# A hybrid decoder trunk: the sampled rows' mixers at the end of the mixing stage, the gating's gate half ahead of its other half

## The chip, the cores and the metric

One Trainium2 chip; the kernel runs on one of its cores. The metric is the device time of one execution in microseconds (us), the median of three runs. One launch computes two layers for 512 prompt rows and for 32 sampled rows (8 sequences of 4 tokens with 2048 cached positions each).

## The reference

Each layer normalises x, projects it from 1024 to 2048 columns, hands these to four mixers of width 256, joins their outputs in one projection of 1024 to 1024, and adds the normalised result to x. A SwiGLU network of inner width 2816 follows.

```python
def hybrid_layer(x, pos, conv_prev, pool_prev, attend, lam_init, p):
    h = rms_norm(x, p['g_mix_pre'])
    z = h @ p['w_in']
    a, ga, u, vb, q, k, v, xd = jnp.split(z, IN_SPLITS, axis=-1)
    ya, conv_new = conformer_conv(a, ga, conv_prev, p['conv_w'], p['conv_b'], p['conv_ln_g'], p['conv_ln_b'])
    yb, v_rows = chunk_sgu(jax.nn.gelu(u, approximate=False), jax.nn.gelu(vb, approximate=False),
                           p['sgu_w'], p['sgu_b'], p['sgu_ln_g'], p['sgu_ln_b'])
    o = attend(q, k, v, lam)
    yc = (rms_norm(o, p['attn_sub_g'], LN_EPS) * (1.0 - lam_init)).reshape(B_, T, D_C)
    yd, pool_new = pool_mix(xd, pool_prev, pos, p['pool_w'], p['pool_scale'])
    mix = jnp.concatenate([ya, yb, yc, yd], axis=-1) @ p['w_out']
    x = x + rms_norm(mix, p['g_mix_post'])
    gate, up = jnp.split(rms_norm(x, p['g_ffn_pre']) @ p['w_gu'], 2, axis=-1)
    x = x + rms_norm((jax.nn.silu(gate) * up) @ p['w_down'], p['g_ffn_post'])
```

`conformer_conv` is a causal depthwise convolution of 31 taps over `a * sigmoid(ga)`, a LayerNorm and a swish; `chunk_sgu` multiplies u by a 128x128 lower-triangular mixing of the LayerNormed v, plus a bias; `attend` is differential attention, for the sampled rows over their paged cache; `pool_mix` takes means over 2, 4, 8 and 16 positions. The sampled rows continue from `state_conv` (30 rows) and `state_pool` (15 rows) of each sequence.

## The kernel before, in words

Everything is float32, and each product of two float32 matrices is three matmuls of rounded parts (`whi`/`wlo` for weights, `xhi`/`xlo` or `y` for activations; L194 on ScalarE casts the high part of a 128x1024 piece, L197 takes the low part on VectorE, some on GpSimd). Program order per engine is fixed beforehand by a scheduler that lists the generated instructions by their data and by a priority; `urgent` flows get a higher one.

A layer has two stages.

**Mixing** (`mixing`): the input projection runs as 16 units of 24 matmuls, in blocks of 256 columns in the order of the list `order` (conv's two halves, k, q, v of attention, the pooling's 1792, the gating's u at 512 and v at 768). Prompt columns are 256 wide per half, and each second half carries the 32 sampled rows too (288 wide), evicted into `zs`. While blocks come in, the mixers run as generator flows that `advance` steps: `conv` (60 tap steps, L427, on VectorE, then transposes L450, LayerNorm, L458, L460 to L462), `attention`, `gating` (weights `wn` transposed by L578 and masked into `wt`, bias by `wt,sgr`; Gelu L593 and L594 over both halves; v transposed by L600 and LayerNormed into `vn` by L602; product `wt,vn`; L612 and L615 finish it) and `pooling`. The hi/lo halves of the results, `ya`, `yb`, `yc`, `yd`, are made by L351 and L352. PSUM is split among the tags `ps` (3 banks), `acc` (2), `s` (2) and `oT` (1); `gating`'s products use `acc`.

**Feed-forward** (`prompt` as main flow, `sample` in the background): `project_last` multiplies by w_out in eight turns of 24 matmuls 128x512, (token tile, half) in the order of `W_OUT_TURNS`, the 128-row pieces of the 1024 in the order of `W_OUT_ORDER`. The matmuls of the first turns stand in program order among the last steps of the mixing stage, as their `y` and weights come. Each turn ends in a copy L1285, a square L1289 and, on GpSimd, a product with the gain L1290; after the second half of a tile `finish` makes its norm (L1300, the root by L177 and L178, L1308, the square L1313, L1315) and turns it feature-major (L239, L241, L242), from which w_gu and w_down are computed. When all four tiles are turned, `share["turned"]` is set.

`sample` first steps `sample_conv`, `sample_gate` and `sample_pool` in a pool of their own, `smx`. `sample_conv` builds the 34 rows of each sequence in `scx` and adds 31 taps for two channel halves on VectorE: two steps L883 and 60 steps L886 of 128x32 per layer, and then a LayerNorm (L892 to L902). With `turned`, `sample_attention` opens its own pool, loads its tables (`sc`, `se`, `gsub`), spreads the queries (`rep`, `qs` by 32 copies L958), computes the new keys' scores, and then goes through the pages: gathers `kr` (L1000) and `vr` (L1030) by indirect DMA from GpSimd's queue, transposes `kt` (L1003) on VectorE, products `sx<-kt,qs` on TensorE. `sample_ffn` follows.

The lines that the steps below touch, word for word:

```python
W_OUT_ORDER = (6, 7, 0, 1, 2, 3, 4, 5)
            for f in (2, 0):
                S.activation(uv[:, f:f + 2], uv[:, f:f + 2], AF.Gelu)
            S.activation(zs[:, 4:8, :], zs[:, 4:8, :], AF.Gelu)
                V.scalar_tensor_tensor(a[:, c], ext[:, c, :, t:t + 4], pf[:, 8 + 2 * t + c:9 + 2 * t + c], a[:, c],
                                       op0=ALU.mult, op1=ALU.add)
```

## Time and profile before

| | us |
|---|---|
| median of three runs | 1465.84 (1464.1 to 1468.32) |
| the profiled execution, its own time | 1470.1 |
| its span | 1468.2 |
| TensorE busy | 1393.0 (95%) |
| VectorE busy | 816.3 (56%) |
| ScalarE busy | 490.4 (33%) |
| GpSimd busy | 253.9 (17%) |

All rows below are from this one execution; their times count from the start of its span. A busy TensorE is not one at its peak, as the ends of its matmuls are modelled. The granted clock (PEclk) is a share of full speed, in which one level is 2.4 GHz and the other 1.2 GHz.

### The profile page before, as it was taken

The page shows a single profiled execution, that of the slowest core. Times are in us where ns is not written, and L with a number is a line of the kernel's source. Part 1 is how long each engine was busy: PE and PEld are TensorE (multiplying, and loading weights), DVE is VectorE, ACT ScalarE, POOL GpSimd, SP SyncE. Part 2 cuts the span into 40 slices and gives each one's busy share as a digit, 9 for nine tenths or more (in the row PEclk, how much of TensorE's full clock was granted, in tenths as well). Part 3 has the DMA queues.
Part 4 walks back from the last instruction along what each step waited for, and adds up shares of the span by engine and source line. Part 5 has one row for each costly group of instructions (what it writes and reads, how often), then busy time and mean ns, then how long its engine had stood idle before and what let it go on. Part 6 is the DMA issues. An engine that isn't in the chain of part 4 may idle for free.

```text
span 1468.2 us, 22964 instructions
## 1 busy us (share of the span) xinstructions
PE 1393.0 (95%) x9274; PEld 1085.7 (74%) x9274; DVE 816.3 (56%) x1624; ACT 490.4 (33%) x972; POOL 253.9 (17%) x271
## 2 busy tenths in 40 slices
PE   6999798989999999999989997989899999999997
PEld 6988677856676777777779886787566677777775
DVE  4997577866424323433669856867564333333344
ACT  4345444322224221222333464433222332222231
POOL 1000245443300000000210004434342000000003
PEclk9999998999999999999999999999999999999999
DMA  6220336786859731323432213378767596213132
GB/s 206 93 87 30 131 117 213 257 299 230 286 177 292 238 137 58 104 69 128 152 115 73 73 53 109 128 244 299 274 235 266 182 299 210 100 58 115 58 133 90
DMA packets 155204, 235.60 MB, mean 160 GB/s; under 512 B 8880, under 2 KB 116410, under 8 KB 155098
## 3 DMA queue, kind: packets, MB, share of 16 engines
q1 hardware_dynamic: 136522, 166.76, 34.8%
q0 software_dynamic: 18432, 67.12, 12.8%
q8 instruction: 73, 1.20, 0.3%
q14 instruction: 33, 0.27, 0.1%
q10 hardware_dynamic: 144, 0.26, 0.0%
HBM read 222.07 MB, written 12.04 MB: 159 GB/s over the span
## 4 chain that ended last, share of the span: by engine, by line
PE 73%; DVE 8%; issue 7%; DMA 6%; POOL 3%; ACT 2%; another core or an unknown queue 0%; SPq 0%; POOLq 0%; DVEq 0%; ACTq 0%
PE acc L128 57%; PE sx L128 8%; DMA kr<-in_cache_k_dram,ik 4%; PE ps L128 2%; PE s L128 2%; DVE sca L886 2%; POOL vr L1030 1%; DVE wlo L197 1%; PE oT L128 1%; POOL kr L1000 1%; DVE m L1315 1%; ACT whi L194 1%; POOL rsw L178 1%; DMA rws<-in_w_gu_dram 1%; PE ps L518 1%
## 5 line engine op out<-in xcount | busy, mean ns | idle before, releaser
L128 PE MATMUL acc<-xhi,whi 128*128 128x512 f32 (+2 forms) x1152 | 409.5, 357 | 3.7 <-issue 1.7
L128 PE MATMUL acc<-xlo,whi 128*128 128x512 f32 (+2 forms) x1152 | 406.7, 353 | 4.2 <-DVE xlo L242 3.2
L128 PE MATMUL acc<-xhi,wlo 128*128 128x512 f32 (+2 forms) x1152 | 407.1, 354 | 0.4 <-issue 0.2
L197 DVE TENSOR_TENSOR wlo<-raw,whi 128x1024 fp32r<-128x1024 f32 x172 | 216.6, 1265 | 198.8 <-ACT whi L194 193.0
L194 ACT CAST whi<-raw 128x1024 fp32r<-128x1024 f32 x178 | 184.3, 1048 | 362.9 <-PE acc L128 320.8
L128 PEld LDWEIGHTS acc<-xhi,whi 128*128 128x128 f32 x1152 | 219.7, 191 | 47.5 <-issue 14.2
L128 PEld LDWEIGHTS acc<-xlo,whi 128*128 128x128 f32 x1152 | 219.9, 191 | 35.8 <-issue 5.7
L128 PEld LDWEIGHTS acc<-xhi,wlo 128*128 128x128 f32 x1152 | 219.6, 191 | 34.6 <-issue 7.9
L128 PE MATMUL acc<-whi,h 128*128 128x512 f32 x704 | 224.7, 396 | 0.6 <-issue 0.6
L128 PEld LDWEIGHTS acc<-whi,h 128*128 128x128 f32 x704 | 131.3, 188 | 44.5 <-issue 11.2
L128 PE MATMUL acc<-wlo,h 128*128 128x512 f32 x352 | 138.4, 395 | 0.0
L1290 POOL TENSOR_TENSOR m<-m,g_g_ffn_post 128x512 f32<-128x512 f32 x14 | 20.2, 1449 | 511.2 <-ACT junk L1289 511.2
L1003 DVE STREAM_TRANSPOSE kt<-kr 128x1024 f32<-128x1024 f32 x64 | 78.3, 1234 | 47.4 <-DMA kr<-in_cache_k_dram,ik 26.9
L1000 POOL DMA_INDIRECT kr<-in_cache_k_dram,ik x64 | 70.3, 1099 | 109.8 <-DVE kt L1003 85.3
L427 DVE SCALAR_TENSOR_TENSOR cacc<-hext,pf,cacc 128x512 f32<-128x512 f32 x120 | 86.9, 745 | 0.8
L128 PEld LDWEIGHTS acc<-wlo,h 128*128 128x128 f32 x352 | 66.1, 188 | 18.0 <-issue 4.6
L1030 POOL DMA_INDIRECT vr<-in_cache_v_dram,iv x64 | 60.5, 945 | 84.7 <-PE sx L128 67.0
L1359 DVE SCALAR_TENSOR_TENSOR th<-th,acc 128x512 f32<-128x512 f32 (+1 forms) x46 | 29.6, 644 | 78.9 <-PE acc L128 78.9
L178 POOL TENSOR_TENSOR rsw<-rsw,mhalf 128x1 f32<-128x1 f32 (+2 forms) x62 | 38.5, 628 | 172.0 <-DVE rsw L177 169.1
L128 PE MATMUL sx<-kt,qs 128*32 128x128 f32 x1024 | 49.3, 278 | 9.3 <-issue 8.6
L554 POOL TENSOR_TENSOR rse<-e,mhalf 128x8 f32<-128x8 f32 x4 | 7.5, 1879 | 257.4 <-DVE e L552 257.4
L1361 ACT CAST h<-th 128x512 fp32r<-128x512 f32 (+1 forms) x48 | 27.9, 582 | 66.5 <-DVE th L1359 58.9
(422 smaller groups left out, 1835.9 us busy)
## 6 DMA issues: line engine op xcount, KB each, us to landing
...
```

The lines of the kernel that those rows point to most:

```text
L128: T.matmul(out, lhsT, rhs, start=start, stop=stop)
L178: G.tensor_tensor(y, v, mhalf[:P, :n], op=ALU.pow)
L194: S.copy(hi, src)
L197: eng.tensor_tensor(lo, src, hi.bitcast(F32), op=ALU.subtract)
L427: V.scalar_tensor_tensor(a, hext[c][:, t:t + SEQ], pf[:, 8 + 2 * t + c:9 + 2 * t + c], a, op0=ALU.mult, op1=ALU.add)
L886: V.scalar_tensor_tensor(a[:, c], ext[:, c, :, t:t + 4], pf[:, 8 + 2 * t + c:9 + 2 * t + c], a[:, c], op0=ALU.mult, op1=ALU.add)
L1000: G.indirect_dma_start(out=kr, out_offset=None, in_=ck, in_offset=bass.IndirectOffsetOnAxis(ap=ik[:, s, bg:bg + 1], axis=0))
L1003: V.transpose(kt, kr)
L1030: G.indirect_dma_start(out=v.rearrange("p t e -> p (t e)"), out_offset=None, in_=cv, in_offset=bass.IndirectOffsetOnAxis(ap=iv[:, s, a:a + ...
L1290: (V if (t, half) == (3, 1) else G).tensor_tensor(m[t][:, hs], m[t][:, hs], gain[:, hs], op=ALU.mult)
L1359: V.scalar_tensor_tensor(th[:, :n], th[:, :n], 0.5, ou[:, :n], op0=ALU.mult, op1=ALU.mult)
L1361: S.copy(hh, th[:, :n])
```

## The change

It has four parts.

1. The gating's v half (block 768) is projected ahead of the pooling's 1792, and u (512) last. `gating` starts after v: Gelu of v alone, LayerNorm, product; then it waits for "u", takes u's Gelu, and finishes. Its weights `wn` are loaded into the tile of the norm, "xn", whose other user `vn` comes later. The conv's flow becomes urgent for its tail.
2. `sample_conv`, `sample_gate` and `sample_pool` run at the end of `mixing`, in tiles that attention no longer needs (its `q` and `k` tiles and the ring "p"). Their six loads per layer go out from GpSimd's queue in place of SyncE's. The 62 steps by taps become four products 128x496 (windows by taps), four reductions over the taps, and two additions of the bias.
3. A new pool `sqa` holds what the sampled attention needs before the pages: `sample_queries` makes `rep`, the new keys' scores and `onew` before "turned"; `sample_attention` keeps the `qs` copies and the pages.
4. `W_OUT_ORDER` starts with attention's pieces (4, 5) and has the gating's (2, 3) last.

```diff
-W_OUT_ORDER = (6, 7, 0, 1, 2, 3, 4, 5)
+W_OUT_ORDER = (4, 5, 0, 1, 6, 7, 2, 3)
...
+            (768, [(6, ev_copy(uv[:, 2], 6)), (7, ev_copy(uv[:, 3], 7))]),
             (1792, [(14, ev_copy(dext[0], 14, 1.0, 15)), (15, ev_copy(dext[1], 15, 1.0, 15))]),
             (512, [(4, ev_copy(uv[:, 0], 4)), (5, ev_copy(uv[:, 1], 5))]),
-            (768, [(6, ev_copy(uv[:, 2], 6)), (7, ev_copy(uv[:, 3], 7))]),
...
+            urgent.append(flow["conv"])
+            yield
             o = ps()
...
-            wn = mp.tile([128, 4, 128], F32, tag="t512", bufs=3, name="wn")
+            wn = mp.tile([128, 4, 256], F32, tag="xn", bufs=1, name="wn")[:, :, :128]
...
-            for f in (2, 0):
-                S.activation(uv[:, f:f + 2], uv[:, f:f + 2], AF.Gelu)
-            S.activation(zs[:, 4:8, :], zs[:, 4:8, :], AF.Gelu)
+            S.activation(uv[:, 2:4], uv[:, 2:4], AF.Gelu)
+            S.activation(zs[:, 6:8, :], zs[:, 6:8, :], AF.Gelu)
...
+                yield
+            while "u" not in done:
+                yield
+            S.activation(uv[:, 0:2], uv[:, 0:2], AF.Gelu)
+            S.activation(zs[:, 4:6, :], zs[:, 4:6, :], AF.Gelu)
+            for c in range(2):
                 tf = uv[:, 2 + c, :]
                 V.tensor_tensor(tf, tf, uv[:, c, :], op=ALU.mult)
...
         while active:
             advance(1)
+        active += [sample_conv(l, mp), sample_gate(l, mp), sample_pool(l, mp, pw)]
+        while active:
+            advance(1)
+    def spare(mp, tag, n):
+        return mp.tile([128, SEQ], F32, tag=tag, name="sm_" + tag)[:, :n]
+    def spare_p(mp):
+        return mp.tile([128, SEQ], F32, tag="p", bufs=PB, name="smp")
...
-        SY.dma_start(st, A["state_pool"][l].rearrange("s t c -> (s t) c"))
+        G.dma_start(st, A["state_pool"][l].rearrange("s t c -> (s t) c"))
...
-        for t in range(1, CW):
-            for c in range(2):
-                V.scalar_tensor_tensor(a[:, c], ext[:, c, :, t:t + 4], pf[:, 8 + 2 * t + c:9 + 2 * t + c], a[:, c],
-                                       op0=ALU.mult, op1=ALU.add)
+            k = pf[:, 8 + c:9 + c]
+            taps_ = bass.AP(k.tensor, k.offset, [k.ap[0], (0, 4), (0, 4), (2, CW)])
+            for hf in range(2):
+                e = ext[c][:, 4 * hf:4 * hf + 4]
+                win = bass.AP(e.tensor, e.offset, [e.ap[0], (34, 4), (1, 4), (1, CW)])
+                pr = spare_p(mp)[:, :16 * CW].rearrange("p (s t j) -> p s t j", s=4, t=4)
+                V.tensor_tensor(pr, win, taps_, op=ALU.mult)
+                V.tensor_reduce(a[:, c, 4 * hf:4 * hf + 4], pr, axis=AX, op=ALU.add)
+                yield
+            V.tensor_scalar(a[:, c], a[:, c], pf[:, c:c + 1], None, op0=ALU.add)
...
-        with tc.tile_pool(name=f"smx{l}", bufs=1, reuse_waits="tile") as mp:
+        with tc.tile_pool(name=f"sqa{l}", bufs=1, reuse_waits="tile") as qp:
             yield
-            flows = [sample_conv(l, mp, sp), sample_gate(l, mp, sp), sample_pool(l, mp, sp, PW[l])]
-            while flows:
-                for fl in list(flows):
-                    if next(fl, 0) == 0:
-                        flows.remove(fl)
-                yield
+            pre = yield from sample_queries(l, sp, qp)
             while "turned" not in share:
                 yield
-        with tc.tile_pool(name=f"att{l}", bufs=1, reuse_waits="tile") as ap:
-            yield from sample_attention(l, sp, ap, ys, share)
+            with tc.tile_pool(name=f"att{l}", bufs=1, reuse_waits="tile") as ap:
+                yield from sample_attention(l, sp, qp, ap, ys, share, *pre)
```

Three places of the order, first layer. TensorE around the gating's product `wt,vn`, before and after (`ya` and `yb` are the outputs of conv and gating, 128x288 a matmul of the input projection):

```order
L128 MATMUL acc<-wlo,ya 128x512
L128 MATMUL acc<-whi,ya 128x512 x2
L128 MATMUL acc<-wt,vn 64x128 x16
L128 MATMUL acc<-whi,yb 128x512
L128 MATMUL acc<-wlo,yb 128x512
```

```order
L128 MATMUL acc<-xhi,wlo 128x288
L128 MATMUL oT<-pt,vtok 64x128
L128 MATMUL acc<-xhi,whi 128x288
L128 MATMUL acc<-wt,vn 64x128 x8
L128 MATMUL oT<-pt,vtok 64x128 x7
L128 MATMUL acc<-xlo,whi 128x288
L128 MATMUL acc<-xhi,wlo 128x288
L128 MATMUL acc<-xhi,whi 128x288
L128 MATMUL acc<-xlo,whi 128x288
L128 MATMUL acc<-xhi,wlo 128x288
L128 MATMUL acc<-wt,vn 64x128 x8
```

The product, split in two, stood between the out-projection's matmuls and now stands between those of the input projection.

ScalarE behind the hi/lo of the mixers' outputs, before and after (`sm_` and `smp` are the sampled mixers' tiles, L926 the end of the sampled conv's LayerNorm, L194 the casts of w_out's second half, L1285 and L1312 the same copy of a turn's result):

```order
L351 CAST ya<-cacc_466 128x512
L351 CAST ya<-cacc_827 128x512
L351 CAST yb<-uv 128x512 x2
L194 CAST whi<-raw 128x1024 x4
L1285 COPY m_2038<-acc 128x512
L1285 COPY m_2039<-acc 128x512
```

```order
L351 CAST ya<-cacc_466 128x512
L351 CAST yb<-uv 128x512 x2
L887 COPY sm_k0l<-ps 128x4x30
L887 COPY sm_k1h<-ps 128x4x30
L351 CAST ya<-cacc_827 128x512
L810 COPY smp<-ps 120x256
L899 COPY smp<-ps 120x256 x2
L835 ACTIVATE zs<-ps,pf_84 128x32 x2
L926 ACTIVATE zs<-ps,pf_84 128x32 x2
L194 CAST whi<-raw 128x1024 x4
L1312 COPY m_2187<-acc 128x512
```

The four casts stood right behind `yb`, and now behind the sampled mixers' copies and L926.

VectorE in the output projection before (`sca` the sampled conv, `x_t` and `m` the first prompt tile's norm), and after where the sampled conv now stands (L912 and L913 its products and reductions, L197 the low part of weights for which ScalarE's casts come first):

```order
L883 TENSOR_SCALAR sca<-scx,pf_84 128x32 x2
L1308 SCALAR_TENSOR_TENSOR x_t<-m_2038,rsw,x_t 128x1024
L886 SCALAR_TENSOR_TENSOR sca<-scx,pf_84,sca 128x32 x8
L177 TENSOR_SCALAR rsw<-sumt 128x1
L886 SCALAR_TENSOR_TENSOR sca<-scx,pf_84,sca 128x32 x5
L1315 SCALAR_TENSOR_TENSOR m_2038<-x_t,rsw,g_g_ffn_pre 128x1024
L886 SCALAR_TENSOR_TENSOR sca<-scx,pf_84,sca 128x32 x2
L1300 TENSOR_TENSOR sumt<-sumt 128x1
L886 SCALAR_TENSOR_TENSOR sca<-scx,pf_84,sca 128x32 x2
```

```order
L829 SCALAR_TENSOR_TENSOR sm_q1h<-sm_q1h,cst,sm_k1l 128x32
L912 TENSOR_TENSOR smp<-sm_k0l,pf_84 128x496 x2
L912 TENSOR_TENSOR smp<-sm_k1h,pf_84 128x496 x2
L913 TENSOR_REDUCE sm_k0h<-smp 128x16 x4
L915 TENSOR_SCALAR sm_k0h<-sm_k0h,pf_84 128x32 x2
L345 BN_STATS bn<-ps 32x6
L346 BN_AGGR ag<-bn 32x2
L177 TENSOR_SCALAR rsw<-ag 32x1
L921 TENSOR_SCALAR sm_k0h<-ps,ag,rsw 32x256
L197 TENSOR_TENSOR wlo<-raw,whi 128x1024 x2
```

The steps by taps stood among the norm's steps, and the new products stand ahead of all of them.

## Rows read from the trace of the kernel before

**Rows 1.** The page: busy time by engine, and the chain by line.

```profile
PE 1393.0 (95%) x9274; PEld 1085.7 (74%) x9274; DVE 816.3 (56%) x1624; ACT 490.4 (33%) x972; POOL 253.9 (17%) x271
...
PE acc L128 57%; PE sx L128 8%; DMA kr<-in_cache_k_dram,ik 4%; PE ps L128 2%; PE s L128 2%; DVE sca L886 2%; POOL vr L1030 1%; DVE wlo L197 1%; PE oT L128 1%; POOL kr L1000 1%; DVE m L1315 1%; ACT whi L194 1%; POOL rsw L178 1%; DMA rws<-in_w_gu_dram 1%; PE ps L518 1%
```

**Rows 2.** Stretches: length, busy (xinstructions) PE, PEld, DVE, ACT, POOL; clock, DMA share, GB/s.

```profile
156.10:186.40 30.30, 22.66 (x127) 17.26 (x127) 20.34 (x52) 13.34 (x21) 10.74 (x14) 0.89 0.38 124
...
216.70:243.30 26.60, 17.74 (x110) 15.27 (x109) 26.17 (x56) 14.08 (x31) 12.89 (x13) 0.87 0.46 155
243.30:300.00 56.70, 56.44 (x538) 47.94 (x538) 41.37 (x104) 19.46 (x36) 27.65 (x27) 0.97 0.82 281
300.00:340.00 40.00, 34.97 (x279) 23.82 (x280) 21.68 (x39) 9.30 (x17) 14.09 (x15) 0.91 0.76 271
```

**Rows 3.** Timeline, TensorE: start, us, work [idle before <-releaser].

```profile
180.90 0.50 PE L128 MATMUL acc<-whi,yb 128*128 128x512 f32 x1 [2.71 <-ACT yb L351]
...
186.48 0.40 PE L128 MATMUL acc<-whi,yd 128*128 128x512 f32 x1
...
913.91 0.40 PE L128 MATMUL acc<-whi,yd 128*128 128x512 f32 x1
```

**Rows 4.** Timeline, TensorE, in the output projection and its end.

```profile
223.16 1.11 PE L239 MATMUL sx<-cst,m 128*128 128x128 f32 x4 [3.43 <-DVE xlo L242]
...
232.33 0.28 PE L128 MATMUL acc<-xhi,whi 128*128 128x256 f32 x1
...
243.30 1.09 PE L239 MATMUL sx<-cst,m 128*128 128x128 f32 x8 [2.63 <-DVE m L1315]
...
966.86 0.87 PE L239 MATMUL sx<-cst,m 128*128 128x128 f32 x6 [1.70 <-DVE m L1315]
```

**Rows 5.** Timeline, VectorE and then GpSimd, 218 to 223 us.

```profile
218.94 3.56 DVE L886 SCALAR_TENSOR_TENSOR sca<-scx,pf,sca 128x32 f32<-128x32 f32 x2
...
220.11 2.34 POOL L197 TENSOR_TENSOR wlo<-raw,whi 128x1024 fp32r<-128x1024 f32 x1
```

**Rows 6.** By source line: ns min/median/max, first and last start.

```profile
L886 DVE SCALAR_TENSOR_TENSOR sca<-scx,pf,sca x120: 230/240/2392, 207.0 to 958.5; 128x32 f32<-128x32 f32 x120
...
L655 DVE SCALAR_TENSOR_TENSOR wn<-wn,cst,dext x4: 730/730/732, 115.8 to 860.2; 128x497 f32<-128x497 f32 x4
```

**Rows 7.** Groups of instructions, TensorE, 161 to 178.3: busy, mean ns | idle.

```profile
L128 PE MATMUL acc<-wt,vn 128*64 128x128 f32 x32 | 2.3, 298 | 0.0
L600 PE MATMUL acc<-cst,uv 128*128 128x128 f32 x8 | 1.7, 297 | 1.9 <-DVE vn L602 1.4 <-DVE bsg L590 0.5
...
L128 PE MATMUL acc<-wt,sgr 128*64 128x128 f32 x8 | 1.1, 292 | 0.7 <-POOL wt L581 0.7
...
L578 PE MATMUL acc<-cst,wn 128*128 128x128 f32 x4 | 0.6, 272 | 0.0
```

**Rows 8.** A stretch, columns as in Rows 2.

```profile
147.00:156.10 9.10, 9.10 (x75) 8.42 (x73) 2.62 (x3) 6.75 (x13) 0.92 (x1) 1.00 0.34 119
```

**Rows 9.** Timeline, ScalarE, 149 to 152 us.

```profile
149.55 1.28 ACT L593 ACT_TABLE_LOAD   x1
150.84 1.06 ACT L593 ACTIVATE uv<-uv 128x1024 f32<-128x1024 f32 x1
```

**Rows 10.** Timeline, VectorE, the last hi/lo step of `ya`.

```profile
171.51 0.68 DVE L352 TENSOR_TENSOR ya<-cacc,ya 128x512 fp32r<-128x512 f32 x1
```

**Rows 11.** Timeline, TensorE, then ScalarE: sampled conv's LayerNorm's ends.

```profile
240.28 0.38 PE L892 MATMUL ps<-cst,sca 128*32 128x128 f32 x2
...
249.38 0.65 ACT L900 ACTIVATE zs<-ps,pf 128x32 f32<-128x32 f32 x2 [0.15 <-issue]
```

**Rows 12.** Timeline, GpSimd, VectorE, TensorE: first gather, `kt` and use.

```profile
245.55 1.20 POOL L1000 DMA_INDIRECT kr<-in_cache_k_dram,ik  x1 [0.19 <-issue]
...
255.45 1.23 DVE L1003 STREAM_TRANSPOSE kt<-kr 128x1024 f32<-128x1024 f32 x1
...
263.69 0.64 PE L128 MATMUL sx<-kt,qs 128*32 128x128 f32 x14
```

108 lines of the change are left out of this document (57 added, 51 removed).

## The prediction

> **What bounds the kernel now.** The page comes first. TensorE is busy for 95% of the span; of the chain that ended last 57% is its products with `acc`, and the one VectorE line of the sampled rows in it, L886 (`sca`, their convolution), has 2% [rows 1]. There is little to win but the places where TensorE stands still, and the table of stages finds them [rows 2]: the change of stage at 156.1 to 186.4 us (22.66 busy of 30.30, granted clock 0.89), the end of the output projection at 216.7 to 243.3 (17.74 of 26.60, clock 0.87, with VectorE busy for 26.17) and the sampled attention at 300 to 340 (34.97 of 40.00). Then the timeline says what TensorE waits for. The input projection ends at 156.1; an idle stretch of 2.71 us for `yb` ends at 180.90, and the third turn of the output projection (token tile 0, second half) starts at 186.48, 30.4 us after the projection's end [rows 3]; in layer 2 it starts at 913.91. Later TensorE waits 3.43 us for VectorE's `xlo`, and 2.63 us for the last `m`; the turn of that `m` to feature-major, on which the whole feed-forward stage hangs, is at 243.30, in layer 2 at 966.86 [rows 4]. What VectorE did meanwhile: two `sca` steps of 128x32 took 3.56 us beside GpSimd's `wlo` of 2.34 [rows 5], where such a step has a median of 0.24 [rows 6].
>
> **The sum is made in differences.** The profiled execution took 1470.1 us, 4.3 more than the median of 1465.84; I add the difference to the median. What a measurement of this kernel can tell from no change is 0.3%, 4.4 us. Four terms follow, each per layer.
>
> **1. The input projection gets longer: +9 us (4.6 to 14).** The gating's v half now comes ahead of the pooling's block, so its transposes and products stand between the projection's matmuls. Moved in are L578 with 0.6 us, `wt,sgr` 1.1, L600 1.7 and `wt,vn` 2.3, which ran at the lower of the clock's levels and counts half: 4.6 [rows 7]. That is the lower bound, every wait hidden by attention's products in other banks. The rest comes from the `acc` banks: there are two, the projection fills them in turn, and the order now puts nine gating products into them, each of which holds its bank until another engine has read it. In the same rows five such trips (four of L600, one of `wt,sgr`) cost 1.9 + 0.7 us of idling, 0.5 each; nine are 4.7, which makes 9.3. At twice that they make 14, the upper bound. I take 9, since VectorE, which reads most of them, was busy for only 2.62 of the projection's last 9.10 us [rows 8].
>
> **2. From the projection's end to the third turn: +0.5 (-4 to +4).** What the gating leaves behind the u block is short: a table load of 1.28, Gelu of 1.06 [rows 9], the product with u and the hi/lo pair. Alone it would bring `yb` over 10 us sooner than the 24.8 of before. But ScalarE's order puts the casts of w_out's second half (four of L194) behind all of the sampled rows' mixers, up to L926, and TensorE's order puts L918 and L924 ahead of the third turn. So that turn waits for a chain: the conv's tail and `ya`, done 16.1 us after the projection's end before (171.51 + 0.68 [rows 10]); the sampled mixers' small steps, some seven of 0.24, 1.7; four products of 128x496 and four reductions of as many elements, which no row shows and which I take at the nearest, 128x497 with 0.73 [rows 6], 5.8 for the eight (from half of it, if reductions overlap with what stands beside them, to twice, if strided reads cost double); their LayerNorm, whose steps took 9.1 from 240.28 to 249.38 [rows 11], with other work between, so half, 4.6; and three casts, 3.2 at the price of the Gelu of the same shape [rows 9]. That is 31.4 against 30.4; half of that excess I take to overlap: +0.5. What comes off the gating's path is given to the sampled mixers, and TensorE stands idle there as before. The six small loads on GpSimd's queue count nothing: they are issued while the conv's tail runs, 16 us ahead of what needs them; past that, each us late is a us here.
>
> As to tables: the row shows a load of 1.28 us, with Gelu right behind it at 150.84. The Trainium skill, "ScalarE: Activation LUTs", section "What ACT_TABLE_LOAD costs", counts a drain of about 1.38 us more for a switch, which speaks against halving the Gelu (two loads more per layer, one of them on this path); by it this term would be 1.4 longer. The trace shows no such drain, and I go by the row.
>
> **3. The output projection: -9.5 us in layer 1, -5.7 in layer 2 (each 2 either way).** From the third turn to the last `m` it takes 56.8 us before, in layer 2 53.0 [rows 3, 4]. After: six turns of 24 matmuls at 0.229 are 33.0 (the 24 from 180.90 to 186.48 took 5.58, with 0.1 for a slow first one [rows 3]); narrow products 5.9, by three turns of an `m` at 1.09 each [rows 4] and 2.6 for the queries that the early pool brings here; and the last tile's norm. That took 11.0 before (232.33 to 243.30), of which TensorE idled the last 2.63 for an `m` that a busy VectorE made late [rows 4]: 8.4 without. The sum is 47.3. This is what the 60 `sca` steps per layer are worth, beside what they wait for: 120 at 0.24 are 29 us over both layers, and the longest took 2.39 [rows 6]. The upper bound keeps the tail as it was, 2.6 more: GpSimd's products with the gain then set the pace.
>
> **4. The sampled attention: -3 us (-8 to +2).** The first gather is at 245.55, 2.3 us behind the last `m`'s turn; in the new order memset and gathers stand right behind the last prompt row's root, which is ahead of that `m`, so some 2.6 us earlier. The queries' 2.6 us of TensorE work leave the stretch, and VectorE makes the 32 `qs` copies before the first `kt`, not between two. Against this stands a new wait: the first product with keys was 20.4 us behind the last `m` (263.69), and now only 41 narrow matmuls, about 5 us, stand between; keys take 255.45 + 1.23 - 245.55 = 11.1 us from their gather [rows 12]. So 3 to 5 us of idling, and less where what follows is bound by the gathers anyway: DMA was busy for 0.82 and 0.76 of the two stretches [rows 2].
>
> W_OUT_ORDER counts nothing: the matmuls' number stays. Sums: layer 1: 9 + 0.5 - 9.5 - 3 = -3.0; layer 2: 9 + 0.5 - 5.7 - 3 = +0.8; together -2.2: 1463.6.
>
> **The rivals.**
> *A, the projection hides its waits.* Term 1 at its lower bound, 4.6 per layer, gives -2.2 - 8.8 = -11.0: 1454.8. For it: VectorE's 6.5 free us before the projection's end. Against it: two `acc` banks.
> *B, VectorE becomes the bound of the change of stage.* The sampled rows' products meet GpSimd's casts and copies there, and a late VectorE holds ScalarE's casts and with them the third turn. Four products that each wait some 1.5 us (two `sca` steps took 3.56 beside GpSimd, 3 us too many) are 6 us per layer: -2.2 + 12 = +9.8, 1475.6. It decides from 3.3 us per layer on, where the time is 0.3% over. For it: rows 5. Against it: GpSimd was busy for 10.74 of 30.30 there [rows 2]. The Trainium skill, "SBUF — State Buffer", section "SBUF: two separate sides", has a VectorE operation with two SBUF inputs and a GpSimd one that reads SBUF lock each other out for a whole instruction; the trace agrees (3.56 against 0.24 each), and by it the products by taps, with two inputs, are such operations.
> *C, the sampled attention gives nothing.* If the wait for keys takes all of term 4, the sum is -2.2 + 6 = +3.8: 1469.6.
> *D, a table switch costs twice its load,* 1.28 more on each layer's path: -2.2 + 2.6 = +0.4, 1466.2. The row at 150.84 speaks against it; the Trainium skill's rule named at term 2 for it.
>
> **How the numbers follow.** The forecast, with its own spread of 1458 to 1470, has 0.35, A 0.26, B 0.24, C 0.11, D 0.04. Of the forecast 0.14 lies under the bound of 0.3%, 0.16 within it, 0.05 over it. A is faster, B slower but for 0.03, C within but for 0.01 and 0.03 on its sides, D within. Faster 0.41, same 0.30, slower 0.29. A with term 4 at -8 would be under 1446, B with term 2 at its end over 1480; the range is 1446 to 1478, about one in ten left out on each side.
>
> **What would show it.** Right: a projection that ends at about 165; the third turn 30 to 31 us behind it, with ScalarE's L194 as its releaser; 47 us from there to the last `m`, and no small VectorE step in between; a wait of 3 to 5 us of `sx` for `kt`. Wrong: a projection's end before 161 (A), a third turn more than 34 us behind it (B), a last `m` no sooner against the third turn, or a first product with keys that does not wait.

## The result and the profile after

| | before | after |
|---|---|---|
| median of four runs each, one chip | 1467.08 us (1464.1 to 1475.25) | 1507.76 us (1502.87 to 1512.13) |
| the profiled execution, its own time | 1470.1 | 1502.87 |
| its span | 1468.2 | 1501.2 |
| mean granted clock | 0.981 | 0.971 |

The ratio is 1.0285, interval 1.0246 to 1.0323: the change makes the kernel slower by about 41 us, where 1463.6 was forecast and the range ended at 1478. The profiled execution is the lowest of the four runs and shows 33 of them; the other 8 stand in no trace.

The page of the changed kernel, busy time and the chain by line, answers to [rows 1]:

```profile
PE 1419.1 (95%) x9274; PEld 1097.8 (73%) x9274; DVE 805.5 (54%) x1520; ACT 498.1 (33%) x978; POOL 270.6 (18%) x283
...
PE acc L128 63%; PE sx L128 11%; PE ps L128 3%; PE s L128 3%; DMA raw<-in_w_in_dram 1%; PE oT L128 1%; DVE wlo L197 1%; DMA kr<-in_cache_k_dram,ik 1%; ACT whi L194 1%; DMA x_t<-in_x_prompt_dram 1%; PE ps L521 1%; POOL rsw L178 1%; DVE m L1342 1%; PE ps L1042 0%; PE sx L239 0%
```

The steps by taps are gone from the chain and VectorE has 104 instructions fewer, as meant; TensorE issues the same 9274 matmuls and is busy for 26 us longer. The page says no more. Cutting each layer at four matmuls that both kernels have does: the projection's first of 288 columns (96 narrower ones of it run ahead of that) and its last, the first of the third turn, and the first that turns the last `m`. "Rest" runs to the next layer's first cut or, in layer 2, to the last matmul; a control, the kernel before on another chip, stands beside.

| us, layer 1 / layer 2 | projection | to the third turn | out-projection | rest |
|---|---|---|---|---|
| before | 124.1 / 126.3 | 30.6 / 31.0 | 56.8 / 53.0 | 513.3 / 492.4 |
| after | 138.3 / 140.3 | 30.5 / 34.4 | 54.3 / 52.1 | 517.1 / 494.5 |
| after less before | +14.2 / +14.0 | -0.1 / +3.4 | -2.5 / -0.9 | +3.8 / +2.1 |
| forecast | +9 / +9 | +0.5 / +0.5 | -9.5 / -5.7 | -3 / -3 |
| the control | 124.1 / 126.3 | 29.5 / 31.5 | 56.9 / 51.8 | 501.0 / 475.6 |

The differences sum to 34.0, and the first cut lies 0.7 us sooner: 33.3 of the spans' 33.0. Stretches of the changed kernel, columns as in [rows 2]:

```profile
31.10:169.40 138.30, 135.47 (x1029) 120.68 (x1028) 106.36 (x243) 62.09 (x156) 12.48 (x17) 0.98 0.22 70
120.00:124.00 4.00, 4.00 (x31) 3.13 (x30) 2.76 (x8) 3.78 (x7) 1.35 (x1) 1.00 0.06 7
124.00:127.00 3.00, 3.00 (x17) 3.00 (x17) 0.66 (x4) 2.97 (x7) 0.32 (x1) 0.56 0.90 345
130.00:150.00 20.00, 18.35 (x122) 14.16 (x123) 15.52 (x45) 9.41 (x25) 5.36 (x10) 0.96 0.09 23
148.00:151.00 3.00, 2.59 (x12) 2.58 (x13) 2.14 (x6) 1.11 (x2) 0.55 (x1) 0.54 0.00 0
169.40:199.90 30.50, 20.75 (x99) 14.28 (x98) 22.26 (x62) 15.74 (x33) 8.26 (x12) 0.82 0.26 74
198.00:204.00 6.00, 3.26 (x7) 2.27 (x8) 4.16 (x2) 5.49 (x13) 5.95 (x3) 0.50 1.02 313
199.90:254.20 54.30, 49.35 (x268) 40.51 (x269) 37.35 (x70) 25.56 (x55) 26.54 (x21) 0.94 0.53 183
254.20:334.20 80.00, 75.05 (x708) 57.40 (x709) 53.23 (x120) 21.95 (x38) 41.50 (x38) 0.94 0.77 275
...
998.10:1078.10 80.00, 72.67 (x665) 55.58 (x666) 53.01 (x119) 20.57 (x36) 37.73 (x37) 0.94 0.74 264
```

The same view of the kernel before, its projection, out-projection and the first 80 us behind the last turn of layer 1, then those 80 us of layer 2:

```profile
31.70:155.90 124.20, 123.40 (x961) 110.95 (x959) 98.80 (x215) 59.78 (x153) 2.38 (x2) 1.00 0.23 72
186.40:243.30 56.90, 48.04 (x256) 39.36 (x254) 49.64 (x144) 24.57 (x57) 25.23 (x26) 0.94 0.43 144
243.30:323.30 80.00, 76.97 (x742) 61.82 (x743) 58.11 (x137) 26.01 (x48) 36.88 (x37) 0.98 0.80 277
...
966.90:1046.90 80.00, 74.97 (x709) 59.88 (x713) 56.80 (x136) 26.47 (x48) 34.84 (x36) 1.00 0.78 276
```

**The projection.** 68 more matmuls stand in it (52 of gating's, the rest of attention, the conv and the first turns), and it takes 14.2 us more, in layer 2 14.0. The clock was 1.00 all through before; now it falls to the lower level twice, at 124 and at 148 (0.56 and 0.54 in the rows). Over the four us from 124 and from 148 it is 0.57, which is up to 3.4 us lost; in layer 2 it falls once, 0.57 from 865 to 869. TensorE's timeline shows gating's products:

```profile
146.80 0.44 PE L602 MATMUL acc<-cst,uv 128*128 128x128 f32 x2 [0.48 <-ACT uv L374]
148.41 1.97 PE L521 MATMUL ps<-cst,p 128*128 128x128 f32 x8 [1.18 <-DVE p L518]
...
154.01 1.09 PE L128 MATMUL acc<-wt,vn 128*64 128x128 f32 x16
...
156.77 1.09 PE L128 MATMUL acc<-wt,vn 128*64 128x128 f32 x16
```

Between L602's products (also at 128.51, 134.85 and 141.50) 8 to 24 of the projection's matmuls go through, in 5 to 7 us each, where the idle columns show next to nothing. That is what a busy share hides: TensorE counts as busy for 135.47 of 138.30. VectorE was not free here: it is busy for 15.52 of the 20 us from 130 on, where the forecast's row, from the projection's end, had 2.62 of 9.10.

**To the third turn.** TensorE, then ScalarE, at the end of the sampled rows' mixers:

```profile
193.41 0.38 PE L918 MATMUL ps<-cst,sm_k0h 128*32 128x128 f32 x2
195.96 0.34 PE L924 MATMUL ps<-cst,sm_k0h 32*128 32x32 f32 x2 [2.17 <-DVE sm_k0h L921]
199.86 0.80 PE L128 MATMUL acc<-whi,yc 128*128 128x512 f32 x1 [3.56 <-ACT whi L194]
201.54 0.79 PE L128 MATMUL acc<-wlo,yc 128*128 128x512 f32 x1 [0.88 <-DVE wlo L197]
```

```profile
196.34 0.65 ACT L926 ACTIVATE zs<-ps,pf 128x32 f32<-128x32 f32 x2 [3.14 <-PE ps L924]
196.88 3.88 ACT L194 CAST whi<-raw 128x1024 fp32r<-128x1024 f32 x4
```

The chain is the one forecast: the last sampled LayerNorm, then the casts, the turn behind the third of them. It starts with the clock at its lower level, 0.50 from 198 to 204.

**The out-projection.** Waits in it, TensorE, then VectorE, then GpSimd:

```profile
217.08 1.07 PE L128 MATMUL ps<-zs,qm 128*32 128x32 f32 x16 [0.98 <-ACT kn L971]
...
234.26 0.66 PE L239 MATMUL sx<-cst,m 128*128 128x128 f32 x4 [1.12 <-DVE m L1342]
```

```profile
215.68 0.23 DVE L299 TENSOR_TENSOR lq<-lq 128x64 f32<-128x64 f32 x1 [5.72 <-DMA lq<-in_lambda_k_dram]
...
240.59 4.12 DVE L197 TENSOR_TENSOR wlo<-raw,whi 128x1024 fp32r<-128x1024 f32 x2 [0.79 <-ACT whi L194]
244.63 2.32 DVE L1342 SCALAR_TENSOR_TENSOR m<-x_t,rsw,g_g_ffn_pre 128x1024 f32<-128x1024 f32 x1
```

```profile
236.77 5.71 POOL L197 TENSOR_TENSOR wlo<-raw,whi 128x1024 fp32r<-128x1024 f32 x2 [0.25 <-ACT whi L194]
```

The 60 steps by taps no longer delay the last `m`, but the queries now stand there, with a wait for a small load (`lq`), and VectorE meets GpSimd again: two L197 take 4.12, where one has a mean of 1.28 over the run.

**The sampled attention.** GpSimd's first gather, then TensorE's first products with keys; they answer to [rows 12]:

```profile
254.90 1.33 POOL L1027 DMA_INDIRECT kr<-in_cache_k_dram,ik  x1 [1.30 <-ACT h L1388]
```

```profile
260.98 0.64 PE L128 MATMUL sx<-kt,qs 128*32 128x128 f32 x16
262.86 1.07 PE L128 MATMUL sx<-kt,qs 128*32 128x128 f32 x13 [0.92 <-DVE kt L1030]
264.97 0.66 PE L128 MATMUL sx<-kt,qs 128*32 128x128 f32 x3 [1.05 <-issue]
...
269.25 1.01 PE L128 MATMUL sx<-kt,qs 128*32 128x128 f32 x10 [0.77 <-issue]
```

The first product with keys is 6.8 us behind the last turn, not 20.4, and the products come in pieces with waits between them. In the first 80 us 708 matmuls get through instead of 742: TensorE idles for 4.95 instead of 3.03, and the clock is at 0.94 instead of 0.98. In layer 2 it is 665 instead of 709, at 0.94 instead of 1.00.

### The profile page after: what moved, and what is told of

It is laid out like the page before. It is cut to its first block, busy times and chain, and to the rows that moved or that the text cites. A ratio compares the mean times of both kernels' runs of the same rounds, so it can differ in the third digit from the quotient of the medians.

```text
span 1501.2 us, 22975 instructions
## 1 busy us (share of the span) xinstructions
PE 1419.1 (95%) x9274; PEld 1097.8 (73%) x9274; DVE 805.5 (54%) x1520; ACT 498.1 (33%) x978; POOL 270.6 (18%) x283
## 3 DMA queue, kind: packets, MB, share of 16 engines
q1 hardware_dynamic: 135424, 165.81, 33.6%
q0 software_dynamic: 18912, 68.07, 12.4%
## 4 chain that ended last, share of the span: by engine, by line
PE 84%; DVE 4%; issue 4%; DMA 4%; ACT 2%; POOL 1%; SPq 1%; POOLq 0%; DVEq 0%; ACTq 0%
PE acc L128 63%; PE sx L128 11%; PE ps L128 3%; PE s L128 3%; DMA raw<-in_w_in_dram 1%; PE oT L128 1%; DVE wlo L197 1%; DMA kr<-in_cache_k_dram,ik 1%; ACT whi L194 1%; DMA x_t<-in_x_prompt_dram 1%; PE ps L521 1%; POOL rsw L178 1%; DVE m L1342 1%; PE ps L1042 0%; PE sx L239 0%
## 5 line engine op out<-in xcount | busy, mean ns | idle before, releaser
L194 ACT CAST whi<-raw 128x1024 fp32r<-128x1024 f32 x178 | 185.0, 1048 | 378.3 <-PE acc L128 313.3
L197 DVE TENSOR_TENSOR wlo<-raw,whi 128x1024 fp32r<-128x1024 f32 x172 | 218.1, 1275 | 163.2 <-ACT whi L194 143.1
L128 PEld LDWEIGHTS acc<-xhi,whi 128*128 128x128 f32 x1152 | 220.3, 192 | 51.8 <-issue 19.8
L128 PEld LDWEIGHTS acc<-xhi,wlo 128*128 128x128 f32 x1152 | 219.8, 191 | 36.5 <-issue 10.8
L128 PE MATMUL acc<-wlo,h 128*128 128x512 f32 x352 | 137.3, 393 | 0.0
L178 POOL TENSOR_TENSOR rsw<-rsw,mhalf 128x1 f32<-128x1 f32 (+2 forms) x62 | 42.0, 679 | 254.0 <-DVE rsw L177 202.2
L1057 POOL DMA_INDIRECT vr<-in_cache_v_dram,iv x64 | 64.0, 999 | 81.5 <-PE sx L128 63.7
L128 PE MATMUL sx<-kt,qs 128*32 128x128 f32 x1024 | 51.4, 282 | 13.6 <-issue 10.2
L128 PEld LDWEIGHTS sx<-kt,qs 128*32 128x32 f32 x1024 | 32.4, 111 | 30.0 <-issue 21.8
L128 PE MATMUL sx<-vr,pt 128*32 128x256 f32 x512 | 48.3, 383 | 0.0
## 6 DMA issues: line engine op xcount, KB each, us to landing
rws<-in_w_gu_dram SPq DMA_DIRECT2D x40, 512.0 KB
rwo<-in_w_out_dram SPq DMA_DIRECT2D x16, 512.0 KB
rws<-in_w_down_dram SPq DMA_DIRECT2D x16, 512.0 KB
x<-x_t SPq DMA_DIRECT2D x12, 512.0 KB
```

What stands on the lines that cost most here:

```text
L128: T.matmul(out, lhsT, rhs, start=start, stop=stop)
L178: G.tensor_tensor(y, v, mhalf[:P, :n], op=ALU.pow)
L194: S.copy(hi, src)
L197: eng.tensor_tensor(lo, src, hi.bitcast(F32), op=ALU.subtract)
L1057: G.indirect_dma_start(out=v.rearrange("p t e -> p (t e)"), out_offset=None, in_=cv, in_offset=bass.IndirectOffsetOnAxis(ap=iv[:, s, a:a + ...
```

## Experiments

Fifteen kernels ran, on four chips, and chips differ: the kernel before took 1440 us on chip A, 1460 on B, 1441 on C, 1467 on D. So every ratio is to the kernel before on the same chip, and stretches are held against the control above, which ran on C (for A and C), or the profile of before (for B and D). That profile took 10 us more than B's median, so a few us in B's rest say nothing. Theories and their letters are as each expectation puts them.

| kernel | ratio to before, interval | projection | to third turn | out-projection | rest |
|---|---|---|---|---|---|
| A: e1, gating ahead alone | 0.9995 (0.9974 to 1.0016) | 137.9 / 139.2 | 20.7 / 21.5 | 53.2 / 51.7 | 498.3 / 474.5 |
| A: e2, the change, gating back | 1.0162 (1.0128 to 1.0196) | 126.4 / 125.8 | 39.0 / 42.3 | 51.5 / 50.8 | 505.6 / 481.2 |
| A: e3, mixers moved alone | 1.0262 (1.0229 to 1.0295) | 126.4 / 125.8 | 45.0 / 42.9 | 48.0 / 47.3 | 511.1 / 489.3 |
| A: e5, order of w_out alone | 0.9967 (0.9952 to 0.9981) | 124.1 / 126.3 | 29.7 / 27.1 | 54.3 / 54.3 | 498.6 / 477.6 |
| B: f1b, tiles off the ring | 1.0492 (1.0462 to 1.0522) | 137.3 / 142.7 | 33.5 / 29.7 | 57.2 / 56.6 | 528.6 / 499.4 |
| B: f2, e1 with `ps` banks | 1.0055 (1.0017 to 1.0094) | 124.1 / 126.0 | 37.8 / 38.2 | 53.9 / 49.6 | 512.0 / 485.7 |
| B: f3, e5 and products by taps | 0.9967 (0.9942 to 0.9991) | 124.1 / 126.3 | 29.9 / 28.5 | 49.1 / 48.2 | 514.1 / 494.6 |
| B: f4, e3, attention 5 later | 1.0049 (1.0018 to 1.0080) | 127.9 / 125.8 | 43.3 / 43.9 | 48.4 / 47.9 | 506.4 / 480.7 |
| C: g1, the change, attention 9 later | 1.0085 (1.0052 to 1.0118) | 135.7 / 138.2 | 30.7 / 30.6 | 54.2 / 51.4 | 493.9 / 469.1 |
| C: g3, f3, taps first | 1.0132 (1.0108 to 1.0155) | 124.1 / 126.3 | 28.4 / 28.1 | 52.0 / 52.2 | 511.1 / 493.7 |
| C: g4, e1 with three `acc` banks | 1.0108 (1.0077 to 1.0140) | 130.9 / 133.1 | 32.4 / 32.7 | 52.8 / 49.6 | 498.5 / 476.5 |
| D: h1, g3, gathers free | 1.0023 (0.9999 to 1.0047) | 124.1 / 126.3 | 29.7 / 28.1 | 50.7 / 51.9 | 523.8 / 494.9 |
| D: h2, gating back, attention 9 later | 0.9966 (0.9941 to 0.9991) | 127.9 / 125.8 | 38.8 / 41.4 | 51.2 / 51.7 | 504.2 / 480.0 |
| D: h3, e1 and order of w_out | 1.0005 (0.9984 to 1.0027) | 138.3 / 143.1 | 22.2 / 23.6 | 54.7 / 50.2 | 511.7 / 485.2 |

### The parts alone: e1, e2, e3, e5

e1 is the kernel before with part 1 of the change alone; e2 the change without part 1; e3 the kernel before with part 2 alone (no early pool, old `W_OUT_ORDER`); e5 with part 4 alone.

```diff
 e1, against before
+            (768, [(6, ev_copy(uv[:, 2], 6)), (7, ev_copy(uv[:, 3], 7))]),
             (1792, [(14, ev_copy(dext[0], 14, 1.0, 15)), (15, ev_copy(dext[1], 15, 1.0, 15))]),
...
+            while "u" not in done:
+                yield
 e2, against the change
-            (768, [(6, ev_copy(uv[:, 2], 6)), (7, ev_copy(uv[:, 3], 7))]),
...
-            while "u" not in done:
-                yield
 e3, against before
+        active += [sample_conv(l, mp), sample_gate(l, mp), sample_pool(l, mp, pw)]
 e5, against before
-W_OUT_ORDER = (6, 7, 0, 1, 2, 3, 4, 5)
+W_OUT_ORDER = (4, 5, 0, 1, 6, 7, 2, 3)
```

> The kernel before with the gating's v half ahead, and nothing else of the change. Theory G (the gating's products among the projection's matmuls make it longer by 14 us per layer, by held banks and two falls of the clock): the projection ends at 168 to 170 in layer 1, as with the whole change (169.3 against 155.8 before). With no sampled mixers ahead of the third turn, that turn then comes some 20 us behind the projection's end instead of 30, so the whole is +2 to +12 us against the kernel before. Theory S (the projection is longer because the sampled mixers' tiles and urgent flows reach back into it): the projection ends at 155 to 161, and the whole is -15 to -5.

> The whole change with the gating put back to where it was (order of blocks, one Gelu of both halves, its tile, the conv's flow not urgent). Theory G: the projection ends at 155 to 158 and the kernel is 20 to 30 us faster than with the whole change, +8 to +20 against the kernel before, since the third turn still waits for the sampled mixers behind a gating that is late again. Theory S: the projection ends near 169 and the whole stays at +30 or more.

> Only the sampled mixers moved to the end of the mixing stage (with their products by taps); queries, gating and the order of w_out's pieces as before. Theory G: the projection ends at 155 to 158; the third turn comes 40 us or more behind it, 10 later than before, and the out-projection from there on is 5 to 9 us shorter without the steps by taps: 0 to +12 in all. Theory S: the projection ends near 169, +25 or more.

> Only the order of w_out's pieces, attention's first and the gating's last. Both theories: nothing, within 3 us of the kernel before. A rival: with the gating's pieces last the first two turns wait for it with less work beside, or with more; then the third turn moves by some us, and the whole by up to 10 either way.

Stretches of e1, layer 1: projection, to the third turn.

```profile
30.00:167.90 137.90, 135.08 (x1026) 120.34 (x1025) 105.72 (x240) 62.12 (x156) 7.93 (x9) 0.98 0.22 67
167.90:188.60 20.70, 16.41 (x64) 11.10 (x63) 14.73 (x28) 14.88 (x23) 6.25 (x6) 0.92 0.49 168
```

Gating ahead costs the projection its 13 to 14 us by itself, and gives 8.8 and 10.0 of them back before the third turn. In layer 1 the rest comes back in the out-projection (53.2 against 56.9), and the whole is nothing. The change shows none of this return against the kernel before, since the sampled rows' mixers spend it: with them alone the third turn is at 39.0 and 42.3 (e2), and gating ahead takes 8.5 and 7.9 off that. e3 has the mixers without gating ahead and without the early pool: 45.0 and 42.9 to the third turn, and an out-projection of 48.0 and 47.3. That looks like the 47.3 of the forecast, but 2.6 of it were for the queries, which e3 has elsewhere; the forecast's sum for e3 is 44.7. The rest then takes 10 and 14 us more than the control's, though term 4 forecast a gain. e5, which was to count nothing, is 0.33% faster.

### The memory of the mixers' tiles: f1b

In the program's layout the casts of w_out's second half write over the memory of the ring "p", on which the sampled rows' tiles now lie. f1b takes those tiles elsewhere and gives the casts priority.

```diff
-        return mp.tile([128, SEQ], F32, tag="p", bufs=PB, name="smp")
+        turn_p[0] = (turn_p[0] + 1) % 3
+        if turn_p[0] == 2:
+            return mp.tile([128, 4, 256], F32, tag="vtok", name="smv").rearrange("p a b -> p (a b)")[:, :SEQ]
+        return mp.tile([128, SEQ], F32, tag=("q1l", "pb")[turn_p[0]], name="smp")
...
+                with tc.high_priority(URG if first else 0):
```

> The whole change, but the sampled mixers' short-lived tiles lie in three places of the mixing pool that the feed-forward stage's first tiles do not take (q1l, pb, vtok) in place of the ring p, on whose memory the four pieces of w_out's second half are laid, and those pieces' casts have the higher priority. Theory M (the third turn waits because its weights need the memory that the sampled mixers still hold): the casts come right behind the hi/lo of the outputs, and the third turn at 24 to 27 us behind the projection's end instead of 30.5 and 34.4; 8 to 15 us less than the whole change. Rival, order alone: the two transposes of the sampled LayerNorm that stand ahead of the third turn on TensorE wait for the same chain on VectorE, so that with the casts early the turn still comes at 29 to 31 and the whole gains under 5.

It was a miss: 1.0492. TensorE, then VectorE, at the third turn of layer 1:

```profile
200.61 0.39 PE L929 MATMUL ps<-cst,sm_k0h 32*128 32x32 f32 x2 [2.17 <-DVE sm_k0h L926]
200.93 0.80 PE L128 MATMUL acc<-whi,yc 128*128 128x512 f32 x1
208.10 0.80 PE L128 MATMUL acc<-wlo,yc 128*128 128x512 f32 x1 [6.38 <-DVE wlo L197]
```

```profile
200.39 8.79 DVE L197 TENSOR_TENSOR wlo<-raw,whi 128x1024 fp32r<-128x1024 f32 x2
```

The four casts run at 193.77 to 197.65, ahead of the LayerNorm's end instead of behind it, and the turn waits all the same: on TensorE the mixers' last products (L929) stand right ahead of it, so it starts 33.5 us behind the projection's end, and on VectorE its low parts, L197, stand behind the mixers, so that its second matmul waits 6.38 us more. With three tiles in turn the mixers were slower too in layer 1: ScalarE's last step of their LayerNorm (L931, at 201.04) comes 33.6 us behind the projection's end, in the change (L926, at 196.34) 27.0. In layer 2 the turn comes at 29.7, 4.7 sooner than in the change. Most of the loss lies in the out-projection and the rest, and was not taken apart. What memory costs by itself stays open; moving the tiles alone is no cure.

### The banks: f2 and g4

f2 gives gating's products in e1 to the `ps` banks; g4 leaves them in `acc` and gives that a third bank.

```diff
 f2, against e1 (four places)
-            o = acc()
+            o = ps()
 g4, against e1
-MIX_BANKS = (("ps", 3), ("acc", 2), ("s", 2), ("oT", 1))
+MIX_BANKS = (("ps", 2), ("acc", 3), ("s", 2), ("oT", 1))
```

> Only the gating's v half ahead, as in e1, but its products use the three ps banks in place of the two acc banks that the projection fills. Theory B (held acc banks make the projection longer): it ends at 161 to 164 instead of 167.9, and the whole is 6 to 14 us faster than e1. Rival (the added matmuls themselves, and the attention's batches that they break up, with the falls of the clock): it ends at 166 or later, and the whole is within 5 us of e1.

> Only the gating's v half ahead, as in e1, with three acc banks and two ps banks in the mixing stage. Theory B (held acc banks): the projection ends 4 to 9 us sooner than e1's 167.9, with the gating's products still inside it, and the whole is 5 to 15 us faster than e1, if two ps banks are enough for attention. Rival (the products' own time and the clock): it ends at 166 or later.

f2 was not the test it was meant to be: in `ps` gating fell behind the projection altogether (the transposes of `wn` are at 158.97), and the projection's 124.1 is one without gating. g4 keeps gating inside: the stretch is 7.0 and 6.1 us shorter than e1's, about half of its 13.8 and 12.9. This row answers to e1's first:

```profile
35.00:165.90 130.90, 130.32 (x988) 115.34 (x987) 104.10 (x232) 60.17 (x151) 5.71 (x6) 1.00 0.22 70
```

It has 988 matmuls instead of 1026. The bank came from `ps`, and 38 of attention's and the conv's matmuls, 3.9 us of e1's stretch from start to start, came late and stand behind it: 32.4 to the third turn, and the whole is 1.1% slower. The clock also stays at 1.00, where e1 has 0.57 from 123 to 127 and from 147 to 151, up to 3.4 us. These two alone make up layer 1's 7.0. In layer 2 both kernels have one such fall, and 36 moved matmuls were 3.6; some 2.5 of the 6.1 are left for the bank. The end of layer 1's projection comes only 2.0 us sooner than e1's (165.9 against 167.9), as its first units were late (the first cut is at 35.0 against 30.0). How much of the projection's 14 us hangs on the `acc` banks stays open.

### The order of the sampled attention's products: f4, g1, h2

A few empty steps ahead of the sampled attention's pages let more of the feed-forward stage's own matmuls be listed ahead of its first product: 97 narrow ones in g1, f4 and h2, 41 in the change (43 in layer 2), 85 in e3. The first gather stays where it was, 0.7 us behind the last turn in the change, g1 and h2.

```diff
 g1, against the change (f4: 5 steps in e3; h2: 9 steps in e2)
+            for _ in range(9):
+                yield
```

> Only the sampled mixers moved, as in e3, with the sampled attention held back by five steps of the background flow once the prompt rows are turned; about as many as the mixers took there before. Theory O (the attention's products stand too early among the main flow's matmuls, so TensorE waits for gathers): the feed-forward stages take 498 to 502 and 477 to 481 us instead of 511.1 and 489.3, and the whole is 16 to 24 us faster than e3. Rival D (the gathers bound the stage, whenever it starts): they stay at 508 or more, and the whole is no faster than e3 by more than 5 us.

> The whole change with the pages' part of the sampled attention held back by nine steps of the background flow (the early queries took four, five as in f4), so that its first product stands behind 97 narrow matmuls of the last tile's turn instead of 41. Theory O: the feed-forward stages get shorter by 5 to 15 us each, and the whole is 10 to 25 us faster than the whole change; it stays slower than the kernel before by 10 to 30 us, since the projection and the change of stage keep their price. Rival D: within 5 us of the whole change.

> The whole change with gating's gate half back in its old place and the sampled attention's pages held back by 9 steps, as in g1. Against g1 (1.0085) it differs by gating alone. If gating ahead is worth nothing once attention's products are late, as it was by itself (e1, 0.9995), this comes out at 1.006 to 1.011. If the sampled mixers keep gating ahead from giving back what it costs the projection (14 us a layer there, 9 to 10 back behind it in e1, none in the change), gating in its old place has a projection of 124 to 126, 39 to 43 from there to the third turn (e2), 48 to 52 to the last turn, and the whole lands at 1.000 to 1.004.

First 80 us behind the last turn of layer 1, e2 and then g1; the control has 78.06 busy and 770 matmuls, the change, on another chip, 75.05 and 708:

```profile
247.00:327.00 80.00, 74.22 (x728) 59.20 (x728) 55.18 (x123) 22.47 (x40) 42.37 (x39) 0.98 0.83 302
```

```profile
250.50:330.50 80.00, 79.52 (x768) 65.35 (x769) 59.89 (x128) 25.95 (x44) 43.74 (x39) 1.00 0.86 308
```

TensorE's idle time is 5.78 us in e2, 4.95 in the change and 0.48 in g1. The rest of g1 takes 7.1 and 6.5 us less than the control's: a gain as term 4 forecast it is there, once the products wait their turn. Part of it may be luck, as this execution is the fastest of g1's four, 6.6 us under their median. f4 gains 2.1% on e3 (1.0262 to 1.0049) though its first product has only 12 more matmuls ahead, so that count is not all that the steps move; and h2's first 80 us have 76.72 busy with 722 matmuls, no more than before, though its rest is 9.1 and 12.4 shorter. Two edits, each with and without the other, give a square whose ratios read:

| | products early | held back 9 steps |
|---|---|---|
| gating ahead | 1.0285 (the change) | 1.0085 (g1) |
| gating in its old place | 1.0162 (e2) | 0.9966 (h2) |

Holding back is worth 2.0% in either row, 29 us; gating ahead costs 1.2% in either column, 17 us (a difference of two cells is good to about 0.5%). e2, g1 and h2 ran on three chips, so the square holds as far as a ratio carries over from chip to chip, which was not tested. By stretches, from e2 to the change, gating ahead adds 11.9 and 14.5 in the projection, takes 8.5 and 7.9 off the way to the third turn and adds 2.8 and 1.3 in the out-projection. In e1, where it costs nothing, the out-projection is 3.7 and 0.1 shorter instead; that is the clearest difference between the two. For h2 my two guesses were 1.006 to 1.011 and 1.000 to 1.004; it is under both, and under the kernel before.

### The gathers' queue: f3, g3, h1

f3 leaves the sampled mixers in their old place and makes only their 62 steps by taps into products (with e5's order). g3 puts these and the LayerNorm ahead of the new state's write-out, without the empty steps among them. h1 takes that write-out's copies off GpSimd.

```diff
 f3, against e5
-        for t in range(1, CW):
...
+                V.tensor_tensor(pr, win, taps_, op=ALU.mult)
+                V.tensor_reduce(a[:, c, 4 * hf:4 * hf + 4], pr, axis=AX, op=ALU.add)
 h1, against g3
-                G.tensor_copy(f, ext[:, c, 4 * hf:4 * hf + 4, 4:34])
+                S.copy(f, ext[:, c, 4 * hf:4 * hf + 4, 4:34])
```

> The kernel before with the new order of w_out's pieces, and the 62 steps by taps replaced by the four products and four reductions in their old place in the out-projection. Theory V (VectorE's small steps make the norms late there): from the third turn to the last m 48 to 50 us instead of 54.3 and 52.6 with the steps, and 6 to 12 us less in all than e5, unless the sampled attention gives it back. Rival D (the attention stage takes back what comes early, since its transfers are the bound): the same 48 to 50, but the feed-forward stage longer by as much, and the whole within 3 us of e5.

> As f3 (products by taps in their old place, new order of w_out's pieces), but the sampled conv's products and LayerNorm come ahead of its new state's write-out, with whose tiles they shared a ring. In f3 GpSimd's first gather stood behind that LayerNorm's root and started 12 us after the last m instead of 2. Theory Q (the gathers' place in GpSimd's queue took back what the out-projection gained): the first gather starts within 2 us of the last m, the feed-forward stages are 5 to 12 us shorter than f3's 514.2 and 494.6 on a chip of the same speed, and the whole is 8 to 20 us faster than the kernel before. Rival: the gathers bound the stage anyway, within 5 us of e5's gain of 4.

> The copies of the sampled conv's windows (scf) go from GpSimd to ScalarE in g3's kernel; everything else stays. Theory Q (the gathers' place on GpSimd's queue cost the time): the first gather stands right behind the norm's root again, at most 1 us behind the last turn (12.3/14.6 us in f3, 6.8/16.8 in g3), the stretch from the last turn to the layer's end falls from 511.1/493.7 to 495 to 501 / 470 to 478, and the whole is 0.5 to 1.5% below the kernel before... 1.0 to 2.5% below g3 (1.0132), so 0.989 to 1.003. Rival theory (the place of attention's products among the main matmuls, 162 to 180 of them ahead of the first product, is too late as such): the gathers come early, but the stretch stays at 508 or more and the whole at 1.005 to 1.015.

> The kernel before once more, on the chip of these runs, as the measure for their stages: nothing is changed. All theories: the projection 124 and 126 us, from its end to the third turn 30 to 31, from there to the last m 53 to 57, and the feed-forward stages between 495 and 515.

f3's out-projection is 7.7 and 4.8 us shorter than that of before: what the products by taps are worth does not need the mixers moved. (The 52.6 of its expectation counts e5's third turn from its second matmul; from the first it is 54.3.) None of it arrives beyond e5, for the first gather stands behind the sampled LayerNorm's root on GpSimd's queue, 12.3 and 14.6 us behind the last turn where it was 2.2. In g3 it stands behind the copies; GpSimd, layer 2, where the last turn is at 954:

```profile
963.37 0.28 POOL L901 COPY scf<-scx 128x120 f32<-128x120 f32 x1 [8.58 <-PE ps L902]
...
971.01 1.07 POOL L1002 DMA_INDIRECT kr<-in_cache_k_dram,ik  x1 [0.16 <-issue]
```

In h1 the gathers come 1.2 and 0.8 us behind the last turn, and the whole goes from 1.0132 to 1.0023. Layer 2 confirms the queue: its rest was 18.1 us over the control's in g3 and is 2.5 over that of before in h1. Layer 1 does not: 10.5 over still. TensorE there waits for another load, that of the sampled attention's table, which in this kernel is asked for only once that attention begins:

```profile
254.07 3.09 PE L128 MATMUL ps<-zs,se 128*128 128x32 f32 x16 [3.65 <-DMA se<-in_c_samp_dram]
```

That is 3.65 of the 10.5; whether the rest is the other theory of this run, products with keys that come too late, is open. Their first is 31.8 us behind the last turn, but in layer 2, which lost little, 30.0.

### A version that beats both: h3, h2, e5

```diff
 h3, against e1
-W_OUT_ORDER = (6, 7, 0, 1, 2, 3, 4, 5)
+W_OUT_ORDER = (4, 5, 0, 1, 6, 7, 2, 3)
```

> Gating ahead alone (e1, 0.9995) with the change's order of the w_out blocks (0.9967 by itself, e5). If the two add, 0.995 to 0.998, with stretches as in e1 and 1 to 3 us less in the out-projection of each layer. If gating ahead already took the time that the order of w_out saves (both bring the out-projection's start or its tail forward), 0.998 to 1.001.

The two do not add: 1.0005. Why is open: the third turn comes 1.5 and 2.1 us later than in e1, and layer 2's projection takes 143.1 where e1's takes 139.2. What beats the kernel before is e5, one line, at 0.9967; h2 with its moved mixers, early pool and nine steps is at 0.9966, no better than that line alone.

## Why the prediction was wrong

The four terms were to sum to -2.2 and came to 34.0. Of the 36.2 between, term 1 has 10.2, term 2 2.3, term 3 11.8 and term 4 11.9. Term 4 failed in kind; the other three were mis-sized.

**Term 1, the projection: right in kind, mis-sized.** Forecast +9 in a range of 4.6 to 14, measured +14.2 and +14.0. What it took at nothing is the clock, held at 1.00 (up to 3.4 us in layer 1, 1.7 in layer 2), and the other flows' matmuls that came into the stretch (1.1 and 1.8 net, from start to start). Gating's own were put a little low: `wt,vn` was halved as work at the lower level, but the granted clock over 175.9 to 178.2, where it ran before, is 0.88, and at 1.00 it takes 2 x 1.09; by the change's timeline the 52 take 5.2, not 4.6. What is left for the nine trips, 4.5 and 5.3, is 0.5 to 0.6 each, about the 0.5 taken. This is a division by difference: no experiment shows a trip alone. The reason given for the lower value, a VectorE with time to spare, was read from the wrong stretch. Rival A falls.

**Term 2, to the third turn: right in layer 1 (-0.1), 2.9 too low in layer 2.** Mechanism and chain are as forecast, down to L194 as the releaser and to the products: L912 took 0.67 and L913's reductions 0.66 each, where 0.73 was taken, and `ya` was done 17.2 us behind the projection's end, where 16.1 was. What the forecast said in passing, that gating alone would bring `yb` over 10 us sooner, shows in e1, whose third turn comes 8.8 and 10.0 sooner; and the mixers take as much again (9.5 and 10.8 in e2), as it said. By the prediction's own sign, more than 34 us, layer 2 with its 34.4 is rival B's. Rival B had the place right, but not the cause or the price of 6 us per layer: in layer 2 VectorE stands idle 3.26 us ahead of the sampled rows' steps, at 934.07, for a product of TensorE's.

**Term 3, the out-projection: mechanism right, mis-sized.** -9.5 and -5.7 forecast, -2.5 and -0.9 measured. The steps by taps are gone from it, and e3 and f3 show it shorter. Two parts of the 47.3 were too small. The six turns were priced with the clock at its upper level all through, while its mean is 0.94 and 0.93 over the stretches, up to 3.3 and 3.6 us. And the queries of the early pool were priced at 2.6 of TensorE's work: layer 1's timeline has 1.86 at 208.90, 0.38 at 210.60, 1.07 at 217.08 and 1.05 at 228.59, 4.4 in all. That is 5.1 of layer 1's 7.0, and 5.4 where layer 2 misses 4.8; the meetings of VectorE with GpSimd's L197 and the wait for `lq` are not priced.

**Term 4, the sampled attention: wrong sign.** -3 forecast, +3.8 and +2.1 measured. The new wait was seen (41 narrow matmuls ahead of the first product, 3 to 5 us of idling). What was missed is that it does not end with the first pages: products with keys that stand early in an in-order queue hold the main matmuls behind them again and again. The idling in the first 80 us of layer 1 is only 1.9 us more than before, and the lower clock, 0.94 against 0.98, costs 3.2 beside it; 34 matmuls less get done, at 80 / 742 each 3.7 us, close to the 3.8. In layer 2 the same count makes 5.0, against 2.1, so it is no measure of the whole rest. Against g1, with the same gathers, the loss is 10.9 and 8.6 us per layer, and the square has 2.0% for both layers. Rival C, no gain, had the right direction and stopped at zero.

**W_OUT_ORDER** counted nothing and is worth 0.33% by itself (e5), nothing beside gating ahead (h3).

**The table loads, rival D.** ScalarE's row after the u block reads the same as before:

```profile
170.98 1.28 ACT L619 ACT_TABLE_LOAD   x1
172.28 1.06 ACT L619 ACTIVATE uv<-uv 128x1024 f32<-128x1024 f32 x1
```

A load of 1.28 and then Gelu: no more. The drain of about 1.38 us that the Trainium skill, "ScalarE: Activation LUTs", section "What ACT_TABLE_LOAD costs", adds to a switch does not show in this trace either.

**The range.** With every term at its upper bound the sum is 14 + 4 - 6.9 + 2 in layer 1 and 14 + 4 - 3.1 + 2 in layer 2, +30.0, near the 32.8 of the profiled executions. That is luck: terms 3 and 4 came out beyond their own bounds, term 2 below. The range was built as if one term could be bad at a time, and all four were worse than their middle in layer 2, three in layer 1.
